# Stacking DMAs split over two queues, and another order of the first layer's steps, in a four-layer fp32 transformer block on one core

## The chip, the cores and the metric

The program runs on one NeuronCore of a Trainium2 chip, in one launch. The metric is the device time of a run in microseconds (us); the median of several runs is compared. TensorE does the matmuls, VectorE (DVE in the profile), ScalarE (ACT) and GpSimd (POOL) the rest, and SyncE (SP) issues all DMAs of the kernel before.

## What is computed

Two blocks of two layers each on 512 tokens of width 1024, all in fp32 (cut to what matters):

```python
# first layer: gated linear recurrence (RG-LRU)
proj = h @ w_in                                   # 1024 x 2048
gate = gelu(proj[..., :1024], approximate=True)
xc = causal_depthwise_conv(proj[..., 1024:], conv_w, conv_b)   # 4 taps
r = sigmoid(block_diag(xc, w_r) + b_r); i = sigmoid(block_diag(xc, w_i) + b_i)
log_a = 8 * r * log_sigmoid(lam)
u = sqrt(max(-expm1(2 * log_a), 0)) * (i * xc)
hs = linear_scan(exp(log_a), u)
x = x + (hs * gate) @ w_out;  x = x + swiglu(rmsnorm(x))
# second layer: stick-breaking attention, 16 heads of 64; then SwiGLU
# third: global, windowed and memory attention with rope and gates
# fourth: neighbourhood and memory attention with gates; final rmsnorm
```

## The kernel before, in words

**Matmuls in three.** Every fp32 operand is split into a high part, rounded to the type that TensorE reads, and a low part, the rest. A product of two such operands is three matmuls (`mm3`, L169 to L171): high by high, high by low, low by high. For weights `fetch` (L149 to L151) loads a chunk of 128 x 512 by a DMA from SP's queue into one of three buffers, ScalarE rounds it to `wh` (L150), VectorE subtracts to get `wl` (L151); six pairs of buffers let this run ahead of TensorE. One chunk feeds twelve matmuls of 512 columns. For activations `split` (L204 and L206) does the same: a ScalarE cast to the high part, and a subtraction, on GpSimd where it is called with "p".

**The order.** The Python code is written in one order, and a scheduler then places the instructions of each engine; buffers are handed out first in, first out. Each engine and each DMA queue runs its own list strictly in that order.

**The first layer** (`rglru`) runs sixteen steps, `RG_STEPS`, which are also the order in which its weights are fetched (`plan_rglru`). An `x` step makes two tiles of the recurrent branch: 48 matmuls, an evacuation with the row's norm (L423), the convolution's first tap with its bias on GpSimd (L426), three more taps on VectorE (L429) and the split. A `g` step makes the two gates of two tiles: 24 matmuls, tanh and exp on ScalarE (L450, L460, L461), on VectorE L462, L464 and L472, a maximum with zero on GpSimd (L465), a square root on ScalarE (L469) and a scan on VectorE (L473). A `y` step makes one tile of the gate branch: 24 matmuls, evacuation (L479), gelu (square on ScalarE L482, a multiply-add on GpSimd L483, a product on VectorE L484, tanh L485, L486), the product with the scan's result (L489) and the split. `lam_consts` (L351 to L369) is a chain of some thirty tiny VectorE operations once. Before, the eight `y` steps stand almost all behind the gates.

**Stacking.** For scores of heads of 64 the kernel stacks parts on the partition axis: `stack_q` (L545) puts the high and the low half of a head above each other in one tile, `stack_k` (L557) puts the high part twice in one tile and the low part twice in another. Each piece is a DMA of 64 partitions from tile to tile: four for a pair of Q heads, eight for a pair of K heads, 240 in all, all in SP's queue between the weight loads. They are used in stick-breaking attention (`sb_mixer`, eight head pairs), in the third layer (`even_mixer`) and in the fourth (`odd_mixer`, eight pairs).

**A head pair of `sb_mixer`**, as TensorE runs it: transposes of the weights of pair p (L714), the Q projection of pair p+2, the scores of pair p+1 (L665, L666), the products of pair p (L726, L727), the K projection of the next. ScalarE rounds the five transposed tiles (`evac_split`, L620), VectorE subtracts (L621); the scores go through two sigmoids a tile (L676, L677) and on VectorE through a scan and a product (L683, L684).

Of the kernel before, what the change touches and what calls it, by code (L numbers as in the profile page):

```python
# [9 lines left out]
F32 = mybir.dt.float32  # L10
F32R = mybir.dt.float32r
BF16 = mybir.dt.bfloat16
AF = mybir.ActivationFunctionType
ALU = mybir.AluOpType
# [51 lines left out]
class Net:  # L66
# [304 lines left out]
    def plan_rglru(self):  # L371
# [15 lines left out]
            self.chunks(("w_rgo", k), kd)  # L387

    RG_STEPS = [
        ("x", 0), ("x", 1), ("g", 0), ("x", 2), ("g", 1), ("x", 3), ("g", 2), ("y", 0), ("y", 1),  # L390
        ("g", 3), ("y", 2), ("y", 3), ("y", 4), ("y", 5), ("y", 6), ("y", 7),
    ]

    def first_pair(self, st):
# [15 lines left out]
    def rglru(self, st, gain_next):  # L410
        nc = self.nc
        v, act, pool = nc.vector, nc.scalar, nc.gpsimd
        c = self.scr
        first = deque(self.first_pair(st))
        YH, YL, conv, hs = [], [], {}, {}
        for kind, n in self.RG_STEPS:
            if kind == "x":
                xcs, ch, cl = [], [], []
                for mt in range(2):
                    m = 2 * n + mt  # L420
                    ps = first.popleft() if first else self.proj(("w_rg", 8 + m), st["XH"], st["XL"])
                    xbt, xb = self.f()
                    v.tensor_tensor(xb, ps, self.row(st), op=ALU.mult)  # L423
                    self.P.put(ps)
                    xct, xc = self.f()
                    pool.tensor_scalar(xc, xb, self.p("conv_w", 24 + m), self.p("conv_b", m), op0=ALU.mult, op1=ALU.add)  # L426
                    for j in (2, 1, 0):
                        d = 3 - j
                        v.scalar_tensor_tensor(xc[:, d:], xb[:, : 512 - d], self.p("conv_w", 8 * j + m), xc[:, d:], op0=ALU.mult, op1=ALU.add)  # L429
                    self.F.put(xbt)  # L430
                    xcs.append((xct, xc))
                    h, l = self.split(xc, "p")
                    ch.append(h)
                    cl.append(l)
                conv[n] = xcs, ch, cl
                if n == 0:
                    self.lam_consts()
            elif kind == "g":
                xcs, ch, cl = conv.pop(n)
                tr = []  # L440
                for g in range(2):
                    wh, wl = self.weights(("w_gate4", n), 512 * g)
                    for mt in range(2):
                        m = 2 * n + mt
                        ps = self.P.get()
                        for kt in range(2):
                            s = slice((mt * 2 + kt) * 128, (mt * 2 + kt + 1) * 128)
                            self.mm3(ps, wh[:, s], wl[:, s], ch[kt], cl[kt], kt == 0, kt == 1)
                        tt, t = self.f()
                        act.activation(t, ps, AF.Tanh, scale=0.5, bias=c[:, 16 + 8 * g + m : 17 + 8 * g + m])  # L450
                        self.P.put(ps)
                        tr.append((tt, t))
                self.R.put(*ch, *cl)
                keep = []
                for mt in range(2):
                    m = 2 * n + mt
                    (rt, r), (it, i) = tr[mt], tr[2 + mt]
                    xct, xc = xcs[mt]
                    at, aa = self.f()
                    act.activation(aa, r, AF.Exp, scale=c[:, m : m + 1], bias=c[:, m : m + 1])  # L460
                    act.activation(r, r, AF.Tanh, scale=c[:, 8 + m : 9 + m], bias=c[:, 8 + m : 9 + m])  # L461
                    v.scalar_tensor_tensor(i, i, 1.0, xc, op0=ALU.add, op1=ALU.mult)  # L462
                    act.square(xc, aa)
                    v.scalar_tensor_tensor(r, xc, 1.0, r, op0=ALU.add, op1=ALU.mult)  # L464
                    pool.tensor_scalar(r, r, 0.0, None, op0=ALU.max)  # L465
                    self.F.put(xct)
                    keep.append((m, at, rt, it))
                for m, at, rt, it in keep:
                    act.sqrt(rt[:, 0:512], rt[:, 0:512])  # L469
                for m, at, rt, it in keep:  # L470
                    r, i = rt[:, 0:512], it[:, 0:512]
                    v.scalar_tensor_tensor(i, i, 0.5, r, op0=ALU.mult, op1=ALU.mult)  # L472
                    v.tensor_tensor_scan(r, at[:, 0:512], i, 0.0, op0=ALU.mult, op1=ALU.add)  # L473
                    self.F.put(at, it)
                    hs[m] = rt
            else:
                ps = self.proj(("w_rg", n), st["XH"], st["XL"])
                gt, g = self.f()
                v.tensor_tensor(g, ps, self.row(st), op=ALU.mult)  # L479
                self.P.put(ps)  # L480
                qt, q = self.f()
                act.square(q, g)  # L482
                pool.tensor_scalar(q, q, 0.044715, 1.0, op0=ALU.mult, op1=ALU.add)  # L483
                v.tensor_tensor(q, q, g, op=ALU.mult)  # L484
                act.activation(q, q, AF.Tanh, scale=0.7978845608028654)  # L485
                v.scalar_tensor_tensor(g, q, 1.0, g, op0=ALU.add, op1=ALU.mult)  # L486
                self.F.put(qt)
                ht = hs.pop(n)
                v.scalar_tensor_tensor(g, g, 0.5, ht[:, 0:512], op0=ALU.mult, op1=ALU.mult)  # L489
                self.F.put(ht)  # L490
                yh, yl = self.split(g, "p")
                self.F.put(gt)
                YH.append(yh)
                YL.append(yl)
        self.free_norm(st)
        outs = self.start_out([], ("w_rgo",), KD, YH[:5], YL[:5], 3, 4)
        self.start_out(outs, ("w_rgo",), KD, YH[:7], YL[:7], 3)
        nx = self.residual_norm(self.add_residual(("w_rgo",), YH, YL, outs), gain_next)
        self.R.put(*YH, *YL)
        return nx  # L500
# [43 lines left out]
    def stack_q(self, q32):  # L544

        nc = self.nc
        h, l = self.split(q32, "p")
        out = []
        for s in (slice(0, 64), slice(64, 128)):
            t = self.R.get()  # L550
            nc.sync.dma_start(t[0:64].bitcast(F32), h[s].bitcast(F32))
            nc.sync.dma_start(t[64:128].bitcast(F32), l[s].bitcast(F32))
            out.append(t)
        self.R.put(h, l)
        return out

    def stack_k(self, k32):  # L557

        nc = self.nc
        h, l = self.split(k32, "p")  # L560
        out = []
        for s in (slice(0, 64), slice(64, 128)):
            pair = []
            for part in (h, l):
                t = self.R.get()
                nc.sync.dma_start(t[0:64].bitcast(F32), part[s].bitcast(F32))
                nc.sync.dma_start(t[64:128].bitcast(F32), part[s].bitcast(F32))
                pair.append(t)
            out.append(pair)
        self.R.put(h, l)  # L570
        return out
# [1285 lines left out]
```

## Time and profile before

| | |
|---|---|
| median of 3 runs | 1899.28 us (1898.69 to 1900.81) |
| the profiled execution | 1898.13 us, its span 1896.1 us |
| granted TensorE clock, mean | 0.996 |
| busy: TensorE, its weight loads | 1855.3 us (98%), 1545.3 us (81%) |
| busy: VectorE, ScalarE, GpSimd | 1204.7 us (64%), 882.5 us (47%), 318.5 us (17%) |
| stacking DMAs (`r<-r`) | 240 of 128 KB, median 2.5 us from issue to landing |

Matmuls are pipelined: each is listed as busy longer than the distance to the next, so a busy share of 98% does not say that they follow at full rate. The number of matmuls in a stretch of fixed length says that.

### The profile page before, as it was taken

The numbers are of one execution on the slowest core, as the hardware profiler recorded it, in microseconds if no ns is written. First come the engines' busy times: TensorE is split into PE (matmuls) and PEld (weight loads), VectorE is DVE, ScalarE is ACT, GpSimd is POOL, SyncE is SP. The second block draws the span as 40 slices with busy tenths as digits, with TensorE's granted clock in tenths as the row PEclk, the third lists the DMA queues.
The fourth block names the chain that finished last, engine by engine and source line by source line (L and its number), as shares of the span: only waits on it lengthen the run. The fifth ranks groups of instructions, "written<-read, shape, count | busy, mean of one in ns | idle before, by whom it ended". The sixth has DMA issues, their size and how long they took to land. (4 is left out here: it accounts for less than half of the span.)

```text
span 1896.1 us, 25818 instructions
## 1 busy us (share of the span) xinstructions
PE 1855.3 (98%) x9003; PEld 1545.3 (81%) x9003; DVE 1204.7 (64%) x2181; ACT 882.5 (47%) x1709; POOL 318.5 (17%) x370
## 2 busy tenths in 40 slices
PE   9899999999999999999999999999999999999998
PEld 6777888888888888788888888788888888888877
DVE  8886555553335998655554335779897665776753
ACT  5764333333334665533333344456665444545542
POOL 3342000000001221200000131222212411322310
PEclk9999999999999999999999999999999999999999
DMA  5333333333335442333333334322443433545532
GB/s 157 101 106 106 95 99 96 97 97 97 94 95 161 135 139 78 94 96 98 97 97 103 104 114 145 89 73 62 112 113 95 129 96 98 145 138 144 142 95 73
DMA packets 124802, 204.04 MB, mean 108 GB/s; under 512 B 21208, under 2 KB 31192, under 8 KB 124672
## 3 DMA queue, kind: packets, MB, share of 16 engines
q1 hardware_dynamic: 124672, 202.39, 37.0%
q8 instruction: 71, 1.16, 0.3%
q14 instruction: 59, 0.48, 0.1%
HBM read 168.76 MB, written 4.40 MB: 91 GB/s over the span
## 5 line engine op out<-in xcount | busy, mean ns | idle before, releaser
L171 PE MATMUL p<-r,wl 128*128 128x512 f32 (+1 forms) x2216 | 853.7, 385 | 10.3 <-DVE wl L151 10.3
L169 PE MATMUL p<-r,wh 128*128 128x512 f32 (+1 forms) x2216 | 856.9, 387 | 2.0 <-ACT wh L150 1.4
L170 PE MATMUL p<-r,wh 128*128 128x512 f32 (+1 forms) x2216 | 852.7, 385 | 3.0 <-POOL r L206 2.2
L150 ACT CAST wh<-w 128x512 fp32r<-128x512 f32 x608 | 371.4, 616 | 643.3 <-PE p L170 480.3
L151 DVE TENSOR_TENSOR wl<-w,wh 128x512 fp32r<-128x512 f32 x608 | 439.9, 727 | 339.4 <-ACT wh L150 337.0
L171 PEld LDWEIGHTS p<-r,wl 128*128 128x128 f32 x2216 | 417.2, 188 | 96.3 <-DVE wl L151 13.9
L169 PEld LDWEIGHTS p<-r,wh 128*128 128x128 f32 x2216 | 417.0, 188 | 86.0 <-ACT wh L150 4.0
L170 PEld LDWEIGHTS p<-r,wh 128*128 128x128 f32 x2216 | 417.3, 188 | 85.6 <-POOL r L206 4.3
L206 POOL TENSOR_TENSOR r<-f,r 128x512 fp32r<-128x512 f32 x102 | 139.5, 1369 | 455.5 <-ACT r L204 454.7
L204 ACT CAST r<-f 128x512 fp32r<-128x512 f32 x146 | 90.7, 621 | 186.2 <-DVE f L532 65.3
L220 POOL TENSOR_TENSOR f<-f,f 128x512 f32<-128x512 f32 x40 | 56.2, 1412 | 478.2 <-ACT f L214 478.0
L506 DVE TENSOR_TENSOR f<-p,f 128x512 f32<-128x512 f32 x68 | 46.9, 690 | 83.5 <-PE p L171 82.8
L621 DVE TENSOR_TENSOR r<-p,r 128x512 fp32r<-128x512 f32 (+2 forms) x152 | 90.4, 638 | 3.7 <-ACT r L620 3.4
L620 ACT CAST r<-p 128x512 fp32r<-128x512 f32 (+2 forms) x152 | 77.2, 558 | 10.5 <-PE p L1152 5.4
L597 PE MATMUL p<-wh,r 128*128 128x512 f32 (+1 forms) x192 | 71.7, 374 | 0.6 <-DVE f L610 0.6
L599 PE MATMUL p<-wh,r 128*128 128x512 f32 (+1 forms) x192 | 71.4, 372 | 0.0
L598 PE MATMUL p<-wl,r 128*128 128x512 f32 (+1 forms) x192 | 71.3, 372 | 0.0
L530 DVE TENSOR_TENSOR f<-p,f 128x512 f32<-128x512 f32 x44 | 30.4, 691 | 63.6 <-PE p L171 63.6
L509 ACT ACTIVATE f<-f 128x512 f32<-128x512 f32 x68 | 43.0, 633 | 38.6 <-DVE f L506 38.5
L682 POOL MEMSET f<- 128x1 f32 x64 | 5.2, 99 | 313.9 <-DVE f L510 208.3
L965 DVE TENSOR_SCALAR f<-f,s 128x256 f32<-128x256 f32 (+3 forms) x160 | 56.5, 416 | 1.1
L683 DVE TENSOR_TENSOR_SCAN f<-f,f 128x127 f32<-128x127 f32 (+3 forms) x64 | 53.1, 870 | 6.3 <-ACT f L676 6.3
(214 smaller groups left out, 1852.9 us busy)
## 6 DMA issues: line engine op xcount, KB each, us to landing
w<-w_gu SPq DMA_DIRECT2D x176, 256.0 KB, 2.9
r<-r SPq DMA_DIRECT2D x240, 128.0 KB, 2.5
w<-w_d SPq DMA_DIRECT2D x80, 256.0 KB, 2.7
w<-wo_m SPq DMA_DIRECT2D x64, 256.0 KB, 2.9
w<-we_m SPq DMA_DIRECT2D x52, 256.0 KB, 2.9
w<-w_rg SPq DMA_DIRECT2D x32, 256.0 KB, 3.0
w<-w_sqk SPq DMA_DIRECT2D x32, 256.0 KB, 2.9
w<-we_o SPq DMA_DIRECT2D x24, 256.0 KB, 2.6
```

Source lines behind the costliest of these rows:

```text
L150: nc.scalar.copy(h[:, :n], w[:, :n])
L151: nc.vector.tensor_tensor(l[:, :n], w[:, :n], h[:, :n].bitcast(F32), op=ALU.subtract)
L169: mm(out, wh, xh, start=start, stop=False)
L170: mm(out, wh, xl, start=False, stop=False)
L171: mm(out, wl, xh, start=False, stop=stop)
L204: nc.scalar.copy(h, src)
L206: e.tensor_tensor(l, src, h.bitcast(F32), op=ALU.subtract)
L597: mm(o, xh, h[:, s], start=st, stop=False)
L598: mm(o, xh, l[:, s], start=False, stop=False)
L599: mm(o, xl, h[:, s], start=False, stop=sp)
L620: nc.scalar.copy(h[:, :n], ps[:, :n])
L621: nc.vector.tensor_tensor(l[:, :n], ps[:, :n], h[:, :n].bitcast(F32), op=ALU.subtract)
```

## The change

The stacking DMAs that read a high part, 120 of the 240, are issued from ScalarE's queue; those of the low parts stay with SP. In the first layer the `y` steps are spread between the `x` and `g` steps; the convolution's first tap moves from GpSimd to ScalarE; and the gelu's multiply-add on GpSimd goes away, its factor going into ScalarE's square and its addition of one into VectorE's product.

```diff
     RG_STEPS = [
-        ("x", 0), ("x", 1), ("g", 0), ("x", 2), ("g", 1), ("x", 3), ("g", 2), ("y", 0), ("y", 1),
-        ("g", 3), ("y", 2), ("y", 3), ("y", 4), ("y", 5), ("y", 6), ("y", 7),
+        ("x", 0), ("x", 1), ("g", 0), ("y", 0), ("x", 2), ("g", 1), ("y", 1), ("y", 2), ("x", 3),
+        ("g", 2), ("y", 3), ("y", 4), ("g", 3), ("y", 5), ("y", 6), ("y", 7),
     ]
...
-                    pool.tensor_scalar(xc, xb, self.p("conv_w", 24 + m), self.p("conv_b", m), op0=ALU.mult, op1=ALU.add)
+                    act.activation(xc, xb, AF.Identity, scale=self.p("conv_w", 24 + m), bias=self.p("conv_b", m))
...
-                act.square(q, g)
-                pool.tensor_scalar(q, q, 0.044715, 1.0, op0=ALU.mult, op1=ALU.add)
-                v.tensor_tensor(q, q, g, op=ALU.mult)
+                act.activation(q, g, AF.Square, scale=0.044715**0.5)
+                v.scalar_tensor_tensor(q, q, 1.0, g, op0=ALU.add, op1=ALU.mult)
...
             t = self.R.get()
-            nc.sync.dma_start(t[0:64].bitcast(F32), h[s].bitcast(F32))
+            nc.scalar.dma_start(t[0:64].bitcast(F32), h[s].bitcast(F32))
             nc.sync.dma_start(t[64:128].bitcast(F32), l[s].bitcast(F32))
...
                 t = self.R.get()
-                nc.sync.dma_start(t[0:64].bitcast(F32), part[s].bitcast(F32))
-                nc.sync.dma_start(t[64:128].bitcast(F32), part[s].bitcast(F32))
+                q = nc.scalar if part is h else nc.sync
+                q.dma_start(t[0:64].bitcast(F32), part[s].bitcast(F32))
+                q.dma_start(t[64:128].bitcast(F32), part[s].bitcast(F32))
```

What this moves in the engines' lists shows at three places. (In the rows below `w`, `wh` and `wl` are a weight chunk and its parts, `f` fp32 tiles, `p` PSUM banks, `r` split tiles, `par` the parameters.) The first is VectorE's list around the gate step of tiles 2 and 3, from one weight chunk's low part to the next. Before:

```order
L151 TENSOR_TENSOR wl_232<-w_0_220,wh_226 128x512
L464 SCALAR_TENSOR_TENSOR f_216<-f_219,f_216 128x512
L423 TENSOR_TENSOR f_206<-p_118,f_212 128x512
L429 SCALAR_TENSOR_TENSOR f_209<-f_206,par,f_209 128x511
L472 SCALAR_TENSOR_TENSOR f_218<-f_218,f_214 128x512
L472 SCALAR_TENSOR_TENSOR f_213<-f_213,f_216 128x512
L473 SCALAR_TENSOR_TENSOR f_214<-f_215,f_218 128x512
L473 SCALAR_TENSOR_TENSOR f_216<-f_208,f_213 128x512
L151 TENSOR_TENSOR wl_233<-w_1_221,wh_227 128x512
```

Of the change:

```order
L151 TENSOR_TENSOR wl_234<-w_2_222,wh_228 128x512
L479 TENSOR_TENSOR f_207<-p_119,f_212 128x512
L464 SCALAR_TENSOR_TENSOR f_213<-f_219,f_213 128x512
L472 SCALAR_TENSOR_TENSOR f_215<-f_215,f_218 128x512
L472 SCALAR_TENSOR_TENSOR f_208<-f_208,f_213 128x512
L473 SCALAR_TENSOR_TENSOR f_218<-f_206,f_215 128x512
L473 SCALAR_TENSOR_TENSOR f_213<-f_209,f_208 128x512
L151 TENSOR_TENSOR wl_229<-w_0_220,wh_223 128x512
L483 SCALAR_TENSOR_TENSOR f_211<-f_211,f_207 128x512
L151 TENSOR_TENSOR wl_230<-w_1_221,wh_224 128x512
L151 TENSOR_TENSOR wl_231<-w_2_222,wh_225 128x512
```

The evacuation and the tap of the next `x` tile (L423, L429) no longer stand between the two chunks; the evacuation of a `y` tile (L479) does, and behind the scans the chunks follow close on each other.

The second place is ScalarE's list in a head pair of `sb_mixer`, from the rounding of the first transposed tile on (L204 is the cast of K's high part). Before:

```order
L620 CAST r_169<-p_116 128x512
L204 CAST r_167<-f_202 128x512
L620 CAST r_175<-p_118 128x512
L620 CAST r_156<-p_119 128x512
L620 CAST r_177<-p_117 128x512
L620 CAST r_142<-p_121 128x512
L150 CAST wh_227<-w_1_221 128x512
```

Of the change:

```order
L620 CAST r_176<-p_121 128x512
L204 CAST r_177<-f_209 128x512
L620 CAST r_135<-p_122 128x512
L566 DMA r_154<-r_177 64x512
L567 DMA r_154<-r_177 64x512
L566 DMA r_158<-r_177 64x512
L567 DMA r_158<-r_177 64x512
L620 CAST r_170<-p_120 128x512
L620 CAST r_165<-p_115 128x512
L620 CAST r_175<-p_116 128x512
L150 CAST wh_223<-w_0_220 128x512
```

Four DMA issues now stand ahead of the last three roundings.

The third place is the same list a little later, where the cast of Q's high part meets the sigmoids. Of the change (before, the same rows stand there without the two DMAs, and L204 ahead of the first sigmoid):

```order
L676 ACTIVATE f_203<-p_119 128x512
L204 CAST r_156<-f_212 128x512
L677 ACTIVATE f_217<-p_119 128x512
L550 DMA r_155<-r_156 64x512
L550 DMA r_161<-r_156 64x512
L676 ACTIVATE f_206<-p_117 128x512
```

Two issues now stand between the sigmoids of the first score tile and those of the second.

## Rows read from the trace of the kernel before

**Rows 1.** The page, part 1: busy us (share of the span) xinstructions.
```profile
PE 1855.3 (98%) x9003; PEld 1545.3 (81%) x9003; DVE 1204.7 (64%) x2181; ACT 882.5 (47%) x1709; POOL 318.5 (17%) x370
```
**Rows 2.** Windows of 25 us: us, busy and count by engine, clock, DMA, GB/s.
```profile
50.00:75.00 25.00, 23.04 (x100) 18.11 (x98) 20.42 (x26) 21.79 (x34) 12.21 (x9) 1.00 0.31 95
75.00:100.00 25.00, 20.25 (x81) 16.26 (x82) 21.44 (x29) 16.77 (x25) 7.72 (x6) 0.93 0.32 94
100.00:125.00 25.00, 24.01 (x105) 19.29 (x104) 22.70 (x31) 20.49 (x33) 11.13 (x9) 1.00 0.39 117
125.00:150.00 25.00, 23.14 (x98) 17.96 (x98) 19.70 (x25) 11.71 (x21) 10.41 (x9) 1.00 0.30 95
...
200.00:225.00 25.00, 25.00 (x112) 20.70 (x111) 13.43 (x21) 8.09 (x13) 0.00 (x0) 1.00 0.34 99
```
**Rows 3.** TensorE's waits, 24 to 150 us: total us, times, longest.
```profile
PE p L171 <- DVE wl L151: 6.9, 4, 3.7
PE p L170 <- POOL r L206: 1.9, 2, 1.0
```
**Rows 4.** Timeline of TensorE: start us, us, instruction [idle before].
```profile
72.71 0.39 PE L170 MATMUL p<-r,wh 128*128 128x512 f32 x1
72.94 0.39 PE L171 MATMUL p<-r,wl 128*128 128x512 f32 x1
...
73.96 0.40 PE L170 MATMUL p<-r,wh 128*128 128x512 f32 x1
78.05 0.50 PE L171 MATMUL p<-r,wl 128*128 128x512 f32 x1 [3.69 <-DVE wl L151]
```
**Rows 5.** Timeline of VectorE in the same stretch.
```profile
68.92 0.68 DVE L151 TENSOR_TENSOR wl<-w,wh 128x512 fp32r<-128x512 f32 x1
...
73.21 0.75 DVE L429 SCALAR_TENSOR_TENSOR f<-f,par,f 128x511 f32<-128x511 f32 x1 [2.00 <-POOL f L426]
...
75.08 2.33 DVE L473 TENSOR_TENSOR_SCAN f<-f,f 128x512 f32<-128x512 f32 x2
77.33 0.67 DVE L151 TENSOR_TENSOR wl<-w,wh 128x512 fp32r<-128x512 f32 x1
```
**Rows 6.** Lines, GpSimd, 24 to 150 us: busy, mean ns, idle before and releaser.
```profile
L426 POOL TENSOR_SCALAR f<-f,par 128x512 f32<-128x512 f32 x8 | 8.1, 1012 | 19.2 <-DVE f L423 16.2 <-DVE s L362 3.0
L483 POOL TENSOR_SCALAR f<-f 128x512 f32<-128x512 f32 x8 | 7.4, 926 | 15.9 <-ACT f L482 15.7
```
**Rows 7.** Lines, ScalarE, 0 to 175 us: an activation with scale and bias from a tile.
```profile
L460 ACT ACTIVATE f<-f,lamc 128x512 f32<-128x512 f32 x8 | 6.3, 808 | 3.3 <-DVE lamc L367 3.3
```
**Rows 8.** Window of one head pair of `sb_mixer`, columns as in rows 2.
```profile
655.40:674.50 19.10, 19.05 (x107) 15.74 (x106) 18.39 (x30) 12.54 (x25) 4.61 (x11) 1.00 0.49 139
```
**Rows 9.** Timeline of ScalarE in that head pair.
```profile
656.55 0.62 ACT L204 CAST r<-f 128x512 fp32r<-128x512 f32 x1
657.07 2.05 ACT L620 CAST r<-p 128x512 fp32r<-128x512 f32 x4
...
663.41 0.60 ACT L676 ACTIVATE f<-p 128x512 f32<-128x512 f32 x1
```
**Rows 10.** Timeline of VectorE in that head pair.
```profile
657.50 3.07 DVE L621 TENSOR_TENSOR r<-p,r 128x512 fp32r<-128x512 f32 x5
...
663.07 1.96 DVE L683 TENSOR_TENSOR_SCAN f<-f,f 128x127 f32<-128x127 f32 x2 [0.59 <-ACT f L676]
```
**Rows 11.** Timeline of SP's queue there: the issues of K's stacking DMAs.
```profile
658.02 0.47 SPq L566 DMA_DIRECT2D r<-r  x1
658.54 0.59 SPq L567 DMA_DIRECT2D r<-r  x1
659.23 0.54 SPq L566 DMA_DIRECT2D r<-r  x1
```
**Rows 12.** TensorE's waits over the span, those for stacking DMAs.
```profile
PE p L1129 <- DMA r<-r: 2.3, 2, 1.2
...
PE p L1455 <- DMA r<-r: 1.9, 2, 1.2
```
**Rows 13.** Timeline of VectorE, last head pair but one of the fourth layer.
```profile
1795.72 2.59 DVE L621 TENSOR_TENSOR r<-p,r 128x512 fp32r<-128x512 f32 x4
```
**Rows 14.** Timeline of TensorE there: second head's products begin.
```profile
1798.98 0.22 PE L1493 MATMUL p<-r,r 128*128 128x128 f32 x1
```

## The prediction

> **What bounds the kernel now.** I read the busy line of the page first: TensorE 98%, VectorE 64%, ScalarE 47%, GpSimd 17% [rows 1]. So TensorE bounds the kernel as a whole, and a change that gives it no less work can only win where it stands still. Busy shares hide this, since matmuls are pipelined; the counts don't. Where nothing is short, 25 us hold 112 matmuls, one each 0.223 us. The four slices from 50 to 150 us hold 100, 81, 105 and 98, so 12 + 31 + 7 + 14 = 64 are missing: 64 x 0.223 = **14.3 us** lost in the first layer [rows 2]. That is all that its half of the change can give back.
>
> Next, the waits of TensorE in that stretch: 6.9 us in four waits for the low part of a weight chunk from VectorE, 1.9 us in two for a split on GpSimd [rows 3]. The rest of the 14.3 us comes with them: in the slice that holds the longest wait the granted clock was 0.93 of full speed, and it was 1.00 in the others [rows 2]. So TensorE ran partly at the lower of its levels (1.2 and 2.4 GHz) behind the wait, and curing the wait cures that too.
>
> The timelines show how the longest wait comes about. TensorE's matmuls begin 0.23 us apart until 73.96 us, then it stands 3.69 us for a `wl` [rows 4]. VectorE, in order, made one `wl` at 68.92 and the next at 77.33 us, 8.4 us later, while a chunk feeds TensorE only 12 x 0.223 = 2.7 us. Between the two stand the evacuation and tap of the next `x` tile, four operations of the gate step, and 2.00 us of waiting for GpSimd's first tap [rows 5].
>
> **The first layer, part by part.** VectorE's operations take about 0.7 us each, the scans 2.33 for two [rows 5]. An `x` step gives VectorE 4 chunks and 8 operations, 12 x 0.7 = 8.4 us, against 48 x 0.223 = 10.7 us of TensorE. A `g` step gives 8 x 0.7 + 2.33 = 7.9 against 5.4; a `y` step 6 x 0.7 = 4.2 against 5.4. Alternating `x` and `g`, as now, is 16.3 us of VectorE against 16.1 of TensorE: no slack, so each wait of VectorE's own reaches TensorE. With a `y` in each round it is 20.5 against 21.4. The new order therefore has 0.9 us a round to catch up, besides six pairs of buffers for run-ahead.
>
> The moved tap takes from GpSimd 8 x 1.01 = 8.1 us, the dropped multiply-add 7.4 us; these stood in VectorE's chain, ahead of L429 and L484 [rows 6]. ScalarE pays 8 taps, for which the nearest row is an activation with scale and bias at 0.81 us: 6.5 us [rows 7]. It is busy 70.8 of the 100 us from 50 on [rows 2], so this lies beside other work; if that cover were gone it would cost 6.5 us at most. Square and product keep their number and only take in a factor and an addition: 0, hidden in the same way. The splits on GpSimd, for which TensorE waits 1.9 us, stand behind 15.5 us less work.
>
> I take **-12 us**: nearly all of the 14.3, since cause and cure are at the same place; a gate step still meets an `x` step with one or two `y` between, where I leave 2 us. The ends: -14.3 if every wait goes, -7 if half stay. Nothing or a loss is excluded by the 20.5 against 21.4 unless VectorE waits as long on ScalarE's tap as on GpSimd's.
>
> **The DMA issues, second layer.** An issue on SP's queue takes 0.47 to 0.59 us, mean 0.53 [rows 11]. No row shows one on ScalarE. I take the same price there and let it hold the engine, since each engine runs its list in order. A head pair lasts 19.10 us, with VectorE busy 18.39, ScalarE 12.54 [rows 8], so VectorE is close behind TensorE and what delays it shows. SP's queue is relieved of some 6 issues a pair; TensorE has no wait of weight here for a DMA, so I count nothing for that.
>
> Four issues of K now stand ahead of the last three roundings of transposed weights: 4 x 0.53 = 2.1 us. The second rounding starts at 657.07, and four take 2.05, 0.51 each [rows 9]. So it ends at 657.58, the issues at 659.7, the last rounding at 661.2; VectorE's last subtraction (3.07 / 5 = 0.61) at 661.8. Now its five end at 657.50 + 3.07 = 660.6: 1.3 us earlier. Behind them VectorE idles 0.59 us for the sigmoid before its next scan [rows 10], which absorbs that much: 1.3 - 0.6 = 0.7 a pair. With six full pairs (the first and the last of eight lack neighbours) that is **+4 us**. Q's two issues, 1.1 us, stand between the sigmoids of two score tiles, while VectorE has the scan of the first, 1.96 for two, still to do [rows 10]: 0. If that cover fails too, all six issues count: 6 x 0.53 = 3.2, less 0.6, is 2.6 a pair, +16 in all. The low end is 0, where an issue does not hold the engine.
>
> The Trainium skill, "Advanced Engine Details and Errata", section "Sequencer Loop", says that other engine instructions can be read and queued while control work is being run. That is a reason for the low end; by it this term would be 0. No row here shows ScalarE issuing a DMA.
>
> **The DMA issues, third and fourth layer.** TensorE waits for stacking DMAs 2.3 us at L1129 (third layer) and 1.9 at L1455 (fourth) [rows 12]; their sum, 4.2, is the most that a split over two queues can save there. At L1129 a pair is complete only when its low part has landed, and that comes late, behind GpSimd's subtraction: I let the 2.3 stay. At L1455 I let the 1.9 go. The price in the fourth layer: VectorE's four subtractions end at 1795.72 + 2.59 = 1798.31 [rows 13] and TensorE takes up what follows at 1798.98 [rows 14]: 0.67 us of slack. Two issues of 1.06 us ahead of the roundings exceed it by 0.4, seven times: +3. Sum **+1**; ends -2 and +3.
>
> The Trainium skill, "DMA: Bandwidth & Descriptors", section "Issuing engines are not separate DMA queues", speaks against this half: DMAs from different engines share the same DMA engines, and spreading issues saves only issue time. By it the split would save next to nothing, and the sum would be about 2 us higher. The trace so far agrees in that the waits for these DMAs are only 4.2 us of 1896.
>
> **Sum.** -12 + 4 + 1 = -7 against the profiled execution of 1898.13 us, so 1891; that execution lies 1.15 below the median of the runs, 1899.28, so the median after is **1892 us**. A measurement here can tell some 0.2%, 3.8 us: faster is below 1895.5, slower above 1903.1.
>
> **Rivals.** *Issues are free on ScalarE.* If an engine's work goes on while its queue issues, the DMA terms are 0 and -2: -12 - 2 = -14, **1885 us**. For it: ScalarE has 6.6 us idle in a head pair [rows 8]. Against: an issue takes 0.5 us of its queue, and the roundings stand right behind. Chance 0.24.
>
> *Nothing to be measured.* The first layer gives only its low end, -7 (the wait moves on to another weight chunk: three gate steps still stand near an `x` step), and the DMAs cost 5: -2, **1897 us**; with -12 and the DMA issues at some 10 the same comes out. For it: VectorE's budget is still only 0.9 us a round under TensorE's. Against: the two longest causes, the tap on GpSimd and `x` right behind `g`, are both gone. Chance 0.23.
>
> *ScalarE's issues bound the head pairs: slower.* In the second layer all six issues reach VectorE, +16; with +3 in the fourth and -12 in the first layer that is +7, **1906 us**. It decides from a price p a pair with 6p + 3 - 12 over 3.8, p over 2.1 us; my p is 0.7. For it: VectorE has 0.7 us free in 19.1. Against: 0.59 of that stands right behind the subtractions, and ScalarE is a third idle. Chance 0.11.
>
> **How the numbers follow.** The forecast keeps 0.42. Its own ends lie between the others, so the range is made of the terms: low -14.3 - 2 = -16, 1883; high -7 + 11 (p of 1.3, nothing absorbed, is 8, and 3 in the fourth layer) = +4, 1903. That leaves out the slower rival and a few hundredths below. Faster: the forecast but for 0.06, the free issues whole, a little of the third case, 0.62; same 0.27; slower 0.11.
>
> **What would show it.** The windows of 25 us from 50 to 150 would hold 109 to 112 matmuls with the clock at 1.00, and the waits of TensorE for `wl` there would be under 2 us in all; waits of over 5 us, or a longer one at another `g`, make the first term wrong. In ScalarE's list of the second layer the four K issues would take some 2.1 us between two roundings, VectorE would wait for the later roundings, and a head pair would last 19.8 us instead of 19.1; at 19.1 the issues are free, at over 21 the slower rival has it. Waits of TensorE for stacking DMAs in the fourth layer should be gone, those of the third still there. A time above 1903 or below 1883 means that one of the prices is wrong by more than its bounds.

## The result, and the profile after

| | before | changed |
|---|---|---|
| median of the runs | 1899.0 us (1898.69 to 1900.81, 4 runs) | 1909.9 us (1908.08 to 1912.19, 4 runs) |
| ratio | | 1.0058 (95%: 1.0046 to 1.0071) |
| the profiled execution, its span | 1898.13, 1896.1 us | 1912.19, 1910.4 us |

The change made the kernel **slower by 11 us**, 0.58%; 1892 had been forecast, faster by 7. The busy line of the page after answers to [rows 1]: VectorE's work is the same to the tenth of a us, ScalarE has 6.9 us more, GpSimd 15.0 less. Nothing in it tells of 11 us.

```profile
PE 1860.8 (97%) x9003; PEld 1549.9 (81%) x9003; DVE 1204.7 (63%) x2181; ACT 889.4 (47%) x1717; POOL 303.5 (16%) x354
```

The windows of 25 us after, in the first layer (columns as in [rows 2]):

```profile
50.00:75.00 25.00, 25.00 (x112) 20.71 (x111) 20.80 (x28) 20.11 (x31) 10.14 (x7) 1.00 0.30 95
75.00:100.00 25.00, 23.31 (x103) 18.95 (x102) 22.46 (x29) 17.26 (x28) 7.10 (x5) 1.00 0.37 115
100.00:125.00 25.00, 23.01 (x102) 18.71 (x101) 20.30 (x28) 21.41 (x34) 7.60 (x6) 1.00 0.31 97
125.00:150.00 25.00, 21.58 (x82) 16.97 (x81) 20.43 (x27) 14.25 (x24) 5.12 (x4) 0.86 0.27 88
```

112, 103, 102, 82 matmuls: 49 are missing where 64 were. The short slice with the lower clock has moved from the second to the fourth place; it has not gone. TensorE's waits over the whole span after (total us, times, longest), the first six:

```profile
PE p L171 <- DVE wl L151: 9.4, 6, 2.6
PE p L714 <- DVE f L684: 6.8, 11, 0.9
PE p L1455 <- DMA r<-r: 4.1, 3, 2.3
PE p L1129 <- DMA r<-r: 3.7, 2, 2.5
PE p L1455 <- issue: 3.4, 2, 2.3
PE p L1163 <- DVE r L621: 2.9, 5, 1.1
```

The wait for `wl` is still the largest. The second is new: eleven waits in the head pairs of the second layer; before, no wait for L684 was listed. Those for stacking DMAs (L1455, L1129), 1.9 and 2.3 us in [rows 12], have grown to 4.1 and 3.7, with 3.4 beside them.

To place the loss I add up, over each layer, how much later each matmul starts after the one ahead of it than is usual for its form (0.227 us for 512 columns). This takes in the waits and the slow clock behind them. One profiled execution of each, us:

| | 28 to 160 | 575 to 800 (2nd layer) | 1190 to 1520 (3rd) | 1520 to end (4th, output) |
|---|---|---|---|---|
| before | 14.3 | 11.8 | 15.5 | 12.6 |
| changed | 10.9 | 19.7 | 21.2 | 15.8 |
| difference | -3.4 | +7.9 | +5.7 | +3.2 |

These are single executions: where kernels stand in the same order, the sums of the second and the third layer still vary by up to 2 us and the last column's by 3. The row of differences is what was to be explained: a gain of 3 instead of 12, and losses in the layers that stack, clear of this variation in the second and third, hardly so in the fourth.

### The profile page after: what moved, and what is told of

Read it like the earlier page. It is cut to its first block, busy times and chain, and to the rows that moved or that the text cites. A ratio compares the mean times of both kernels' runs of the same rounds, so it can differ in the third digit from the quotient of the medians.

```text
span 1910.4 us, 25723 instructions
## 1 busy us (share of the span) xinstructions
PE 1860.8 (97%) x9003; PEld 1549.9 (81%) x9003; DVE 1204.7 (63%) x2181; ACT 889.4 (47%) x1717; POOL 303.5 (16%) x354
## 5 line engine op out<-in xcount | busy, mean ns | idle before, releaser
L151 DVE TENSOR_TENSOR wl<-w,wh 128x512 fp32r<-128x512 f32 x608 | 438.6, 725 | 347.2 <-ACT wh L150 346.3
L204 ACT CAST r<-f 128x512 fp32r<-128x512 f32 x146 | 90.6, 621 | 181.7 <-DVE f L531 65.3
L621 DVE TENSOR_TENSOR r<-p,r 128x512 fp32r<-128x512 f32 (+2 forms) x152 | 91.4, 639 | 19.8 <-ACT r L620 19.3
L597 PE MATMUL p<-wh,r 128*128 128x512 f32 (+1 forms) x192 | 71.6, 373 | 0.0
L683 DVE TENSOR_TENSOR_SCAN f<-f,f 128x127 f32<-128x127 f32 (+3 forms) x64 | 54.9, 890 | 1.6 <-ACT f L676 1.6
```

Source lines behind the costliest of these rows:

```text
L151: nc.vector.tensor_tensor(l[:, :n], w[:, :n], h[:, :n].bitcast(F32), op=ALU.subtract)
L204: nc.scalar.copy(h, src)
L597: mm(o, xh, h[:, s], start=st, stop=False)
L621: nc.vector.tensor_tensor(l[:, :n], ps[:, :n], h[:, :n].bitcast(F32), op=ALU.subtract)
```

## The experiments

Each was timed beside the kernel before; the second time given is the median of that kernel's runs there. In kernels with an edit that adds lines, line numbers behind it are one higher (L622 for L621, L152 for L151).

**The two halves.** `e1_dma` is the kernel before with only the DMA edits of the change, `e2_rg` with only the first layer's, `e3_order` with only `RG_STEPS`, `e4_ops` with only the tap and the gelu.

> The kernel before with only the DMA split (120 issues on ScalarE's queue). Theory (ScalarE is held while its queue issues): the layers behind the first lose what the trace of the change lost there, some +8 us in the second, +6 in the third, +3 in the fourth: 1899 + 17 = 1916 (1911 to 1920), a head pair of the second layer 20.5 us long, 1.5 us of VectorE's idle behind the rounding. Rival (the first layer gave its -12 and the DMA part cost all the more): 1910 + 12 = 1922 or above. Forecast's price (+5): 1904.

1913.44 us against 1899.18, ratio 1.0079 (1.0062 to 1.0095): **+14**, inside the theory's range. By the sums: +7.5 in the second layer, +5.6 in the third, +2.1 behind it.

> The kernel before with only the first layer's changes (order of steps and the moved operations), all stacking DMAs on SP's queue. Theory: the first layer gives only what its excess over full rate shows in the trace of the change, 19.4 down to 16.0 us: -3.4, 1895.5 (1893 to 1898), with waits of TensorE for wl of some 8 us left at the gate steps. Rival (the step of the forecast): -12, 1887.

1898.16 against 1899.18, ratio 0.9996 (0.9987 to 1.0005): nothing that can be measured, less even than the -3.4.

> Only the new order of the first layer's steps; tap and gelu as before. Theory: the order brings the gain by giving VectorE room (-3, 1896), the tap on GpSimd leaves VectorE some idle time that the room takes up. Rival: without the moved operations the order is worth nothing, 1899, since VectorE still waits 2 us for the tap.

1904.08, ratio 1.0025 (1.0015 to 1.0036): **+5**, slower. Neither reading had that.

> Only the moved operations: first tap on ScalarE, gelu without GpSimd; order of steps as before. Theory: worth little (0 to -1, 1898 to 1899), for what VectorE no longer waits for GpSimd it waits for ScalarE's square root and roundings. Rival: the 2.0 us wait for the tap went at three gate steps, -5, 1894.

1893.12, ratio 0.9969 (0.9959 to 0.9979): **-6**. The rival holds, and my theory that the operations are worth nothing falls. So the first layer is -6 for the operations and +5 for the order, which nearly cancel. VectorE's waits from 28 to 150 us (total us, times, longest), before:

```profile
DVE f L429 <- POOL f L426: 6.2, 7, 2.0
DVE f L484 <- POOL f L483: 3.4, 4, 1.9
DVE f L464 <- ACT f L463: 2.4, 4, 0.8
DVE f L472 <- ACT f L469: 2.1, 3, 1.0
```

and with the operations alone (`e4_ops`):

```profile
DVE f L472 <- ACT f L469: 4.5, 6, 1.3
DVE f L464 <- ACT f L463: 3.1, 4, 1.5
DVE wl L151 <- ACT wh L150: 2.9, 4, 1.2
DVE f L327 <- PE p L171: 2.0, 1, 2.0
DVE f L429 <- ACT f L426: 1.2, 2, 0.9
```

The 9.6 us of waiting for GpSimd are gone; waiting for ScalarE (the gates' squares, the square roots, the roundings) has grown from 6.1 to 12.4, smaller groups counted. VectorE's gain is what is left between them. TensorE's wait for `wl` in 24 to 150 us falls only from 6.9 [rows 3] to 5.1, but the two waits for a split on GpSimd (1.9 us) go.

**The DMA half: which DMAs, and what about them.** The same edit for one kind alone (`f1_k_act`: `stack_k` of the change, 72 DMAs; `g2_q_act`: `stack_q` of the change, 48), for GpSimd's queue, and for half of K in the second layer:

```diff
-            nc.scalar.dma_start(t[0:64].bitcast(F32), h[s].bitcast(F32))
+            nc.gpsimd.dma_start(t[0:64].bitcast(F32), h[s].bitcast(F32))
...
-                q = nc.scalar if part is h else nc.sync
+                q = nc.gpsimd if part is h else nc.sync
```

That is `f2_pool_issue` against `e1_dma`; the first layer is as before in all four. `g3_half_k` against the kernel before (cut; `sb_k` belongs to the second layer):

```diff
-    def stack_k(self, k32):
+    def stack_k(self, k32, act=False):
...
+                q = nc.scalar if act and part is h and s.start == 0 else nc.sync
...
-        K = self.stack_k(k)
+        K = self.stack_k(k, True)
```

> The kernel before with only K's high parts (80 DMAs) issued from ScalarE's queue; Q's stay on SP's. If the held ScalarE is the cause and K's four issues between the roundings its main place: +9 to +11 of the +14 that both gave, 1909; head pair of the second layer 20.2 us instead of 20.5. If the two issues of Q between the sigmoids cost as much per issue: two thirds, the same 9.5, so the length of the head pair tells, with VectorE's idle behind the rounding (1.5 us) kept whole.

1903.53 against 1900.23, ratio 1.0024 (1.0013 to 1.0035), +3 to +5. Smaller than expected, and spread otherwise: by the sums +7.6 in the second layer, all that the split costs there (a head pair lasts 20.53 us, as in the change), +2.3 in the third, and **-4.3 in the fourth**. (K's high parts are 72 DMAs, not 80.)

> The kernel before with only Q's high parts (48 DMAs) on ScalarE's queue. If Q's and K's shares add up: 14.3 - 4.6 = +10, 1909, none of it in the second layer, 3 in the third, 6 in the fourth. If the cost comes from both together (16 DMA engines busy, Q's low parts issued behind K's and the weights): less than +4, 1903 or below.

1908.09 against 1899.52, ratio 1.0043 (1.0029 to 1.0057), +8. The shares of K and Q nearly add up, as the first reading has it. By the sums +1.1 in the second layer, +1.9 in the third, +5.7 in the fourth.

> The same 120 DMAs issued from GpSimd's queue instead of ScalarE's. Theory (held ScalarE): nothing waits between the roundings, so 1899 within 3 us, and a head pair of the second layer 19.1 us. Rival (two queues at a time make the stacking DMAs land later, 4.2 us instead of 2.5, and that is what TensorE waits for): +10 or more, 1909 and above, with the waits for r<-r as in the change. A third outcome, an issue on GpSimd that takes it from its splits: waits for r of GpSimd at L620 or at the stacking DMAs of the low parts, 1902 to 1908.

1918.22 against 1900.23, ratio 1.0103 (1.0088 to 1.0119), **+18**. The number is the rival's (1909 and above), and it separates the layers. In the second the theory holds: a head pair is as long as before. In the third and fourth the sums rise by 9.8 and 5.6, and there the rival holds: behind 1520 us TensorE waits 10.7 us for stacking DMAs, before 1.9.

> The kernel before, in the second layer alone two of K's four high-part issues on ScalarE's queue, those of the first head (16 DMAs). Four cost 7.6 us there, 1.26 a pair, and hold ScalarE 2.0 us. If half of a hold is absorbed by VectorE's idle 0.59 us, as the forecast had it: 1.0 held, 0.4 a pair, +2 to +3. If it passes on in full from the first issue on: half of 7.6, +3.8, 1903. If a short hold is absorbed whole (the rounding that waits is the third of five, and VectorE is still at the second): 0 to +1.5, a head pair of 19.1 to 19.3 us.

1899.92 against 1899.52, ratio 1.0002 (0.9994 to 1.0011): half of the issues cost nothing that can be measured. The third of the three holds.

Head pairs of the second layer, each from TensorE's transposes to the next pair's, columns as in [rows 8]. The change:

```profile
652.49:673.02 20.53, 19.26 (x105) 15.73 (x105) 18.79 (x30) 12.66 (x24) 4.61 (x11) 1.00 0.46 129
```

With two of the four issues (`g3_half_k`):

```profile
653.75:673.04 19.29, 19.08 (x105) 15.75 (x105) 18.40 (x30) 12.64 (x24) 4.59 (x11) 1.00 0.47 137
```

With GpSimd's queue (`f2_pool_issue`):

```profile
655.40:674.50 19.10, 19.05 (x107) 15.73 (x106) 18.39 (x30) 12.54 (x24) 7.64 (x17) 1.00 0.47 138
```

20.53, 19.29, and 19.10 as before. ScalarE's timeline of the change in that pair, which answers to [rows 9] and [rows 11]:

```profile
656.74 0.59 ACT L620 CAST r<-p 128x512 fp32r<-128x512 f32 x1
656.87 0.47 ACTq L566 DMA_DIRECT2D r<-r  x1
657.38 0.61 ACTq L567 DMA_DIRECT2D r<-r  x1
658.02 0.62 ACTq L566 DMA_DIRECT2D r<-r  x1
658.68 0.61 ACTq L567 DMA_DIRECT2D r<-r  x1
659.33 1.57 ACT L620 CAST r<-p 128x512 fp32r<-128x512 f32 x3 [2.00 <-issue]
```

and VectorE's, which answers to [rows 10]:

```profile
657.17 1.27 DVE L621 TENSOR_TENSOR r<-p,r 128x512 fp32r<-128x512 f32 x2
659.95 1.89 DVE L621 TENSOR_TENSOR r<-p,r 128x512 fp32r<-128x512 f32 x3 [1.51 <-ACT r L620]
...
663.55 2.32 DVE L683 TENSOR_TENSOR_SCAN f<-f,f 128x127 f32<-128x127 f32 x2
```

ScalarE stands for 2.00 us between two roundings while its queue issues four DMAs, and VectorE stands 1.51 us behind it. With two issues VectorE waits 0.21:

```profile
659.34 1.88 DVE L622 TENSOR_TENSOR r<-p,r 128x512 fp32r<-128x512 f32 x3 [0.21 <-ACT r L621]
```

So the cause in the second layer is the held ScalarE, and not the landing of the DMAs: from 575 to 800 us they take a median of 2.9 us to land before, 4.2 and 4.3 on the two queues of the change, 4.1 and 4.5 with GpSimd's queue, and with that the pair keeps its length.

In the third and fourth layer it is more than that: the DMAs land later, and there TensorE waits for them. The page's DMA issues of the change (KB each, median us to landing):

```profile
r<-r ACTq DMA_DIRECT2D x120, 128.0 KB, 4.2
r<-r SPq DMA_DIRECT2D x120, 128.0 KB, 4.4
```

Before, the median was 2.5; with GpSimd's queue it is 4.0 and 4.4. Eleven us from K's first issue on, in the last stacking of the fourth layer, before and then with the DMA half alone (`e1_dma`); the last two columns are the busy share of the 16 DMA engines and the GB/s that they moved:

```profile
1793.00:1804.00 11.00, 9.68 (x59) 8.43 (x58) 7.54 (x11) 5.12 (x10) 3.37 (x5) 1.00 0.84 226
```

```profile
1806.80:1817.80 11.00, 9.77 (x61) 8.54 (x59) 6.83 (x9) 4.23 (x9) 4.41 (x6) 1.00 0.95 226
```

The engines are busy for longer, 0.95 instead of 0.84, and move no more. So the second queue brought nothing through faster here. (That no more can go through isn't shown: with Q alone, `g2_q_act`, 262 GB/s were moved in the same stretch.) Now the cast of Q's high part on ScalarE, the issue of its low parts on SP (L552), and the scores of TensorE that need them, from three timelines put together, before:

```profile
1795.29 0.62 ACT L204 CAST r<-f 128x512 fp32r<-128x512 f32 x1
1798.88 0.54 SPq L552 DMA_DIRECT2D r<-r  x1
1800.11 0.60 SPq L552 DMA_DIRECT2D r<-r  x1
1800.75 0.58 SPq L1434 DMA_DIRECT2D f<-nabias  x1
1801.30 0.33 PE L1455 MATMUL p<-r,r 128*128 128x192 f32 x1 [1.24 <-DMA r<-r]
```

and in `e1_dma`:

```profile
1810.84 0.62 ACT L204 CAST r<-f 128x512 fp32r<-128x512 f32 x1
1811.96 0.53 SPq L1435 DMA_DIRECT2D f<-nabias  x1
1813.29 0.33 SPq L149 DMA_DIRECT2D w<-wo_o  x1
1814.18 1.11 SPq L552 DMA_DIRECT2D r<-r  x2
1818.75 0.33 PE L1456 MATMUL p<-r,r 128*128 128x192 f32 x1 [2.18 <-DMA r<-r]
```

The scores begin 0.13 us behind the landing of the first of Q's two low parts, at 1801.17 and 1818.62. A bias tile and a weight load are now issued ahead of the low parts, where before all four of Q's DMAs went ahead of these. But that is not what makes them late: the first low part is issued 3.34 us behind Q's cast, before 3.59. It takes 4.4 us to land instead of 2.3. With K alone on ScalarE Q's DMAs stand behind the bias tile and a weight load as well, the first low part lands in 2.9 us, and the layer gains. TensorE's waits at this line behind 1520 us go from 1.9 us before to 6.8 in `e1_dma`: 4.2 that the view puts down to stacking DMAs, and 2.6 that it calls "issue", which end 0.09 us behind such a landing too. With K alone they are 1.4, with Q alone 1.8. Why two queues together lengthen the landing so much was not tried.

With Q alone the loss of the fourth layer comes another way: Q's two issues hold the roundings of the transposed weights, which TensorE waits for. ScalarE in `g2_q_act`:

```profile
1802.17 1.25 ACTq L551 DMA_DIRECT2D r<-r  x2
1803.46 1.07 ACT L620 CAST r<-p 128x512 fp32r<-128x512 f32 x2 [1.09 <-DMA r<-r]
```

Each issue takes some 0.5 us; the second stands 0.29 us more for the landing of one of K's DMAs, which the view names, and ScalarE stands with it. VectorE's subtraction waits 0.98 us behind that, and TensorE's waits at L1493 and L1494, none before, come to 2.2 us. With K alone, SP's queue has four issues fewer ahead of Q's. TensorE's named waits behind 1520 us then fall from 1.9 to 1.4 us for the stacking DMAs, from 2.3 to 0.6 at L1476 and from 0.6 to nothing at L597: most of the 4.3, though not by what the split was to cure. How the issues bring about the last two was not tried.

In the third layer TensorE's wait for stacking DMAs (L1129) is 2.3 us before and with K alone, 3.7 with Q alone and 3.8 with both; its wait for VectorE's L621 at L1163 is 1.1, 1.1, 1.3 and 2.9. So a part of the loss there comes only with both kinds together, and K's +2.3 and Q's +1.9 are within or hardly above the variation of this sum. Why was not tried.

**A version from the parts.** `g1_ops_k4` takes the operations of `e4_ops` and gives ScalarE's queue K's high parts in the fourth layer alone:

```diff
-    def stack_k(self, k32):
+    def stack_k(self, k32, act=False):
...
+                q = nc.scalar if act and part is h else nc.sync
...
-                got[want] = self.stack_q(x) if kind == "qc" else self.stack_k(x)
+                got[want] = self.stack_q(x) if kind == "qc" else self.stack_k(x, True)
```

> The moved operations of the first layer (order of steps as before) and K's high parts on ScalarE's queue in the fourth layer alone. With K's parts on ScalarE everywhere the excess over full rate behind 1520 us fell from 12.6 to 8.3, and rose by 7.6 in the second layer and 2.3 in the third. Theory (these layers add up): 1893.1 - 4.3 = 1889 (1887 to 1891). Rival (the gain in the fourth layer came from the later phase in which it was entered): 1893.

**1886.84** us against 1899.52, ratio 0.9930 (0.9915 to 0.9945), -13: below both kernels, and the sum behind 1520 us is 8.6, as with K everywhere (8.3). So the theory holds, and the gain is the place's own.

**The first layer: who should make the low parts?** On the base of `e4_ops`, `fetch` gives them to GpSimd for every second or for all of the chunks 8 to 31:

```diff
-        nc.vector.tensor_tensor(l[:, :n], w[:, :n], h[:, :n].bitcast(F32), op=ALU.subtract)
+        e = nc.gpsimd if 8 <= self.fetched - 1 < 32 else nc.vector
+        e.tensor_tensor(l[:, :n], w[:, :n], h[:, :n].bitcast(F32), op=ALU.subtract)
```

> The moved operations alone (first tap and gelu; order of steps as before), and every second weight chunk of the first layer from the first gate step to the last has its low part made by GpSimd. Theory: what is left there is low parts that stand in VectorE's list behind the gates' chain; without half of them the waits for wl go from 5.1 us to 2 or 3 and 1893.1 becomes 1889 to 1891. Rival: GpSimd's list, with the gates' maximum and the splits in it, holds them as long: 1893 or more.

1900.81 against 1900.23, ratio 1.0009 (1.0000 to 1.0018): all of the 6 us lost again.

> As the one before, with the low parts of all 24 chunks from the first gate step to the last made by GpSimd. Theory: no wait for a wl of VectorE is left from 50 to 150 us, 1886 to 1888, if GpSimd (1.4 us for each, 33 us more in 100) keeps up. Rival: the wait moves to GpSimd's wl behind its maximum and its splits: 1893 to 1900.

1908.24, ratio 1.0052 (1.0038 to 1.0066). The rival holds both times. TensorE's waits from 24 to 150 us with all of them on GpSimd:

```profile
PE p L172 <- POOL wl L152: 7.4, 6, 1.7
PE p L171 <- POOL r L207: 2.6, 2, 1.5
PE p L172 <- DVE wl L152: 2.3, 1, 2.3
```

A second list in strict order, with the gates' maximum in it, holds the low parts as the first did, and VectorE then waits 7.8 us for the square roots where it waited 4.5.

**Why the order costs.** `g4_y_behind_x` has the operations and the order x0 x1 g0 x2 y0 g1 x3 y1 g2 y2 y3 g3 y4 to y7.

> The moved operations, and a third order of the first layer's steps: the y steps spread behind the x steps and ahead of the gates (x0 x1 g0 x2 y0 g1 x3 y1 g2 y2 y3 g3 y4 ...), so that an x still follows each of the first three gates but one. Theory: the change's order costs 5 us because the y right behind a gate puts the gelu, its table load and its roundings into ScalarE's list between the gate's square roots and the next roundings, and VectorE waits for ScalarE; with y behind x it costs less than 1 and may give some (1890 to 1894). Rival (any y between the gates costs): 1896 to 1899.

1895.54 against 1899.52, ratio 0.9976 (0.9966 to 0.9985): beside `e4_ops` a cost of 1 to 2.5 us, between the two readings. Then the gelu's work on ScalarE was taken out of both orders:

```diff
-                act.activation(q, g, AF.Square, scale=0.044715**0.5)
-                v.scalar_tensor_tensor(q, q, 1.0, g, op0=ALU.add, op1=ALU.mult)
-                act.activation(q, q, AF.Tanh, scale=0.7978845608028654)
+                v.scalar_tensor_tensor(q, g, 1.0, g, op0=ALU.add, op1=ALU.mult)
```

> The moved operations with the order of before, and the gelu's square and tanh on ScalarE left out (its two VectorE products stay, so the output is another). It is the base for the next run: if the gelu's ScalarE work costs nothing in this order, 1893, else less.

1891.52 against 1899.32, ratio 0.9954 (0.9942 to 0.9966).

> The same with the change's order of steps (the gelu's square and tanh left out too). Theory (the gelu's table load and operations in ScalarE's list behind the gates make the order dear): equal to the run before within 1.5 us, where with the gelu the two orders differ by 5. Rival (the order of the chunks itself: a y step takes two chunks right behind the gate, before VectorE has come through it): still 4 to 5 us more than the run before.

1894.15, ratio 0.9973 (0.9962 to 0.9985). The orders differ by 2.6 (medians) to 3.6 us (ratios) without the gelu's ScalarE work, and by 5 with it. That is neither "within 1.5" nor "still 4 to 5", and each interval reaches some 2.3 us to either side. In the profiled executions the first layer alone says more for the theory: 28 to 160 us, the sums are 6.5 and 6.6 without the gelu's work, and 7.4 (`e4_ops`) and 9.3 (`e2_rg`) with it. The profiled executions of the first two differ by 4.9 us all the same, in later layers, where their instructions stand in the same order; those of the last two differ by 2.1 in all. VectorE's waits for ScalarE from 28 to 150 us are 12.4 in `e4_ops` and 15.1 in `e2_rg`. ScalarE loads as many activation tables in both orders (8 from 20 to 175 us, 1.28 us each), so more table loads are not the reason. That the order costs some 5 us is measured twice, with the old operations and with the new; that ScalarE's gelu between the gates makes it is likely for a part, and the rest **stays open**.

> The moved operations, K's high parts on ScalarE's queue in the fourth layer alone, and the gates' maximum with zero moved from GpSimd to VectorE. VectorE waits 4.5 us for the square root in the first layer, which waits for GpSimd's maximum. Theory (the hop over GpSimd is part of the gates' chain): each gate's chain gets up to 1 us shorter at 0.4 to 0.7 us of VectorE twice, so -1 to -3 against 1886.8. Rival (VectorE has no room): 1887 to 1890.

1887.46 against 1899.32, ratio 0.9938 (0.9924 to 0.9951): the same as `g1_ops_k4` within the intervals. In its profile the first layer's sum falls from 7.4 to 5.0, but the runs don't show a gain.

## Why the prediction was wrong, point by point

**The order of the first layer's steps was the step that failed.** "It is 20.5 against 21.4. The new order therefore has 0.9 us a round to catch up" counts VectorE's busy time over a round and takes it as if work could be shifted freely within the round. The order alone made the kernel 5 us slower. The waits for `wl` come from shorter stretches, at each gate, where three operations and two scans of the gate step stand in line and VectorE waits for other engines between them. My reading, which the runs bear out for a part only: an `x` step behind the gate fills VectorE's waits there with taps of its own; a `y` step brings a gelu that goes through ScalarE as well. The 14.3 us were also explained less well than I took it: the waits that I named leave 5.5 of them open, and a clock of 0.93 over 25 us is 1.8 of these.

**The moved operations were right in kind, and half in size.** VectorE's waits for GpSimd went (9.6 us to 0), and -6 came of it, of the -12 taken for both parts. What I excluded, that VectorE waits "as long on ScalarE's tap as on GpSimd's", did not come at the tap (1.2 us) but at ScalarE's other links (square root 2.1 to 4.5, roundings). I never asked what would be late next there.

**The issues on ScalarE in the second layer: mechanism right, size half.** An issue takes 0.47 to 0.62 us on ScalarE, and four hold it 2.00, where I had 2.1. The term that was too small is "1.3 us earlier", VectorE's delay. It lets one subtraction follow the last rounding; in the trace three, 1.89 us, follow the first late one, and VectorE's five take 4.67 us from first start to last end instead of 3.07: 1.6 later. The absorption, 0.6, came true: the wait of 0.59 ahead of the scan (L683) is gone. So VectorE's idle time in the pair rose by 1.03 (1.74 after, 0.71 before) where I had 0.7. Its busy time rose by 0.40 besides (18.79 against 18.39, the same 30 instructions), which I had not looked for; the score tiles go through it in another order, but that this is the reason isn't shown. Together the pair grew by 20.53 - 19.10 = 1.43; over the layer it is +7.9 instead of +4. Q's two issues were rightly set at next to nothing there: Q alone adds 1.1.

The Trainium skill, "Advanced Engine Details and Errata", section "Sequencer Loop", lets other engine instructions be read and queued while control work is being run. In the trace that hides little on ScalarE: of the 2.42 us that the four issues span, 0.46 lie beside the rounding ahead of them, and the next rounding starts 2.00 us late, "<-issue", right behind the last of the four.

**The third and fourth layer were forecast at +1 and cost some 8.** The third was set at nothing: "I let the 2.3 stay", and no hold was priced there. It cost 5.6, with TensorE's waits at L1129 up from 2.3 to 3.8 and at L1163 from 1.1 to 2.9. In the fourth the step that failed is "At L1455 I let the 1.9 go": it takes a second queue as bringing the DMAs in earlier. They landed later, 4.4 us for Q's first low part instead of 2.3, and the waits there rose to 6.8. The hold itself was near its price: two issues held ScalarE 1.09 us where I had 1.06, and TensorE's waits behind that came to 2.2 with Q alone, where I had 3. That the fourth layer came out near its +1 all the same (+2 to +3) is luck: K alone gave 4.3 there, for which I had no term, and Q alone cost 5.7.

The Trainium skill, "DMA: Bandwidth & Descriptors", section "Issuing engines are not separate DMA queues", was right here: the median from issue to landing, 2.5 us, became over 4 on either queue, and in the last stacking the DMA engines moved 226 GB/s with one queue and with two. It speaks of little gain; the loss comes from the later landing, and from the engine that issues.

**The rivals.** The slower one had the side and nearly the time (1906 for 1909.9) at a chance of 0.11. Its mechanism, ScalarE's issues reaching VectorE, is the one that the runs show in the second layer, but there p came to 1.43 and not to the 2.1 it needed, and the time is luck: it took +16 for that layer and -12 for the first, where 7.9 and about nothing came, and the rest came from two places it did not name, the order of the steps and the third layer. The range ended at 1903, with the first layer at -7 and the DMAs at +11; measured alone, the two halves were -1 and +14.

## What to carry to other kernels

Count an engine's slack at the place where the others wait for it, link by link, and not as busy time over a round: an order that gives a balanced sum can still put two dependent chains on the same engine. A DMA issue cost ScalarE 0.47 to 0.62 us here: two were absorbed, and four between operations that VectorE waits for cost 1.43 us a head pair. The second queue also made the DMAs land later. So put issues on a second queue one place at a time, and look at the landing as well as at the engine that issues. Here one place of three paid (K in the fourth layer), and by the sums a bundle of edits hid a 6 us gain, a 4 us gain and over 20 us of losses.

## What the runs showed that was not expected

Two issues a head pair cost nothing that can be measured, and four 7.6 us: the price does not grow in proportion. With two, the next rounding is there 0.21 us after VectorE has finished the subtractions ahead of it; with four, 1.51 us after. GpSimd, 16% busy over the kernel, was no better a place for issues than ScalarE (+18 against +14, with intervals that touch), and a bad one for the low parts of weights (from -6 to +8). And in the fourth layer K's issues on ScalarE were worth 4 us, though TensorE waited there only 1.9 us for stacking DMAs.
